# Weight blocks of a two-layer decoder trunk: a rounding load and an accumulating load in place of one plain load and two splits

## Chip, cores and metric

The kernel runs on one core of a Trainium2 chip. The metric is the device time of one execution in microseconds. Before the change it is 2004.49 us, the median of 2 runs (2004.17 and 2004.82).

## What is computed

The reference runs two layers (DEPTH = 2) on x of 512 tokens by 1024 features, all in float32. Per layer, cut to what matters:

```
h    = rms_norm(x, pre_norm[l])
proj = h @ w_in[l]            # one projection, its columns cut into ten parts
y_a  = ssd_branch(z_a, xbc, dt_raw, ...)   @ w_a[l]   # Mamba-2 SSD
y_b  = s5_branch(u_b, z_b, ..., w_glu[l])  @ w_b[l]   # S5, with a 1024x1024 GLU
y_c  = mla_branch(c_q, c_kv, k_rope, z_c, ...) @ w_c[l]  # latent attention, w_uq, w_ukv
out  = (sum of sigmoid(gate_i) * y_i) @ w_o[l]
x    = x + rms_norm(out, post_norm[l])
```

Every `@` with a weight is a dense product whose weight is read from DRAM once.

## The kernel before

TensorE multiplies in a rounded 32-bit type (`F32R`). To keep float32 accuracy every operand is held as two parts: hi, the value rounded to F32R, and lo, the value minus hi, rounded in turn. A product is then three matmuls: hi times hi, hi times lo, lo times hi.

Weights come in blocks of 128 partitions by 1024 columns (512 KB; blocks of `w_uq` and `w_ukv` have 512 columns, `w_tail` 384). `weight` (L83 to L99) prepares one block: SP issues the load of the float32 block into `wf` (L95), ScalarE writes hi into `wh` (line 59, called from L96), and VectorE, or every second or third time GpSimd (`lo_pool`, set in the attention and SSD parts), writes `wl` = `wf` - `wh` (lines 71 and 74). `wf`, `wh` and `wl` have two buffers each. `dense` (L101 to L113) then runs 16 matmuls of 128x128 by 128x512 on `wh` (L109, L110) and 8 on `wl` (L112), into one PSUM bank. `w_out` in `mix` does the same for the eight blocks of `w_o`, into tiles of their own (`woh`, `wol`) that stay for the whole of `wout`; two of these eight lie in memory that the merged sums `mg` occupy until then.

In the S5 blocks `weight` is called with a pool of its own (`sp`), once with a list of eight strided pieces of `kpad` (L93) and once with a contiguous block `odr` that the kernel itself wrote to DRAM earlier.

One layer passes through these stages; the times are those of the first layer: norm, attention with the S5 preparation as a filler (0 to 400 us), the product with `w_c` beside the S5 scan on VectorE (400 to 490), the SSD part (490 to 690), the S5 blocks with `w_a` (690 to 820), the GLU and the product with `w_b` (820 to 925), and on to `w_o` (925 to 1005).

The order of the instructions on each engine is made at build time by a scheduler that places the program's instructions one after the other as their operands and buffers come free. At run time each engine keeps that order: an instruction that waits holds up everything behind it on its own engine. DMA issues are instructions of the engine that issues them, and wait there in the same way.

Of the kernel before, what the change touches and what calls it, by code (L numbers as in the profile page):

```python
# [17 lines left out]
L = 2  # L18
T = 512
# [4 lines left out]
# first tile of each part of the input projection, in the host's order  # L24
# [10 lines left out]
class Trunk:  # L35
# [49 lines left out]
    def weight(self, src, n, pool=None):  # L85
        """hi and lo parts of a block of n columns per partition, streamed from DRAM"""
        pool = pool or self.wp
        wf = pool.tile([P, 1024], F32, name="wf", tag="wf", bufs=2)
        wh = pool.tile([P, 1024], F32R, name="wh", tag="wh", bufs=2)
        wl = pool.tile([P, 1024], F32R, name="wl", tag="wl", bufs=2)  # L90
        if isinstance(src, list):
            for rows, x in src:
                self.nc.sync.dma_start(wf[rows, :n].rearrange("p (g k) -> p g k", k=x.shape[-1]), x)  # L93
        else:
            self.nc.sync.dma_start(wf[:, :n], src)  # L95
        self.act_(wh[:, :n], wf[:, :n])  # L96
        self.nw += 1
        (self.gt if self.lo_pool and self.nw % self.lo_pool == 0 else self.tt)(wl[:, :n], wf[:, :n], wh[:, :n].bitcast(F32), ALU.subtract)
        return wh, wl  # L99

    def dense(self, src, rhs, m=P, n=None, main=True):  # L101
        """[m, T] bank of src^T rhs; rhs: (hi, lo) per 128 rows"""
        k = len(rhs)
        wh, wl = self.weight(src, k * m)
        ps = self.bank(main)
        mm = self.nc.tensor.matmul
        o = lambda i: slice(i * m, i * m + m)
        for i, (bh, bl) in enumerate(rhs):
            mm(ps[:m], wh[:, o(i)], bh, start=i == 0, stop=False)  # L109
            mm(ps[:m], wh[:, o(i)], bl, start=False, stop=False)  # L110
        for i, (bh, bl) in enumerate(rhs):
            mm(ps[:m], wl[:, o(i)], bh, start=False, stop=i == k - 1)  # L112
        return ps  # L113

    def proj2(self, l, tiles):
        """two tiles of the projection, first for the first half of the tokens"""
        w = [self.weight(self.a["w_in"][l, t], 1024) for t in tiles]
        ps = [self.bank(True) for _ in tiles]
        for half in range(2):
            tk = slice(256 * half, 256 * half + 256)  # L120
            for (wh, wl), p in zip(w, ps):
                for i, (bh, bl) in enumerate(self.h):
                    o = slice(i * P, i * P + P)
                    self.mm3(p[:, tk], wh[:, o], wl[:, o], bh[:, tk], bl[:, tk], i == 0, i == 7)
        return ps
# [48 lines left out]
    def sincos_small(self, ang, n):  # L174
# [21 lines left out]
        # sin = 2 s c, cos = 1 - 2 s^2  # L196
# [8 lines left out]
    def rsqrt_mean(self, ss, n, scale, eps=EPS):  # L205
        """(scale * ss + eps) ** -0.5 on n columns"""
        v = self.sm.tile([P, n], F32, name="rs_v", tag=f"rsv{n}")
        r = self.sm.tile([P, n], F32, name="rs_r", tag=f"rsr{n}")
        self.ts(v, ss, scale, eps, ALU.mult, ALU.add)
        self.gt(r, v, self.mhalf[:, :n], ALU.pow)  # L210
        return r

    def rsqrt_rows(self, sq, scale):
        """sq [128, T]: sums over partitions -> (scale * sum + eps) ** -0.5 along T, on every partition"""
        nc = self.nc
        ps = self.bank()
        for t in range(4):
            nc.tensor.matmul(ps[:, t:t + 1], sq[:, t * P:(t + 1) * P], self.ones[:, 0:1], start=True, stop=True)
        r = self.rsqrt_mean(ps[:, 0:4], 4, scale)
        dg = self.tmp()  # L220
        for t in range(4):
            self.ts(dg[:, t * P:(t + 1) * P], self.ident, r[:, t:t + 1], None, ALU.mult)
        pr = self.bank()
        nc.tensor.matmul(pr, self.ones, dg, start=True, stop=True)
        return pr

# [1 line left out]
    def s5_prep(self, l, pp):  # L228
# [27 lines left out]
        # f = (abar - 1) / lambda  # L256
# [18 lines left out]
        # coefficients of the scan over blocks: groups 0..31 on the lower half, 32..63 on the upper  # L275
# [25 lines left out]
        def block(b):  # L301
            """inputs in blocks of 8 steps: (step, channel of the group) on partitions; what depends on B and C alone"""
# [49 lines left out]
        def back(b, s, uf, bb, v1, w1):  # L352
# [19 lines left out]
            if s % 2:  # L372
# [3 lines left out]
                # kernel of the steps within a block  # L376
# [32 lines left out]
    def norm_in(self, tt, xt, G):  # L409
        """RMS norm of a tile of tokens (two halves of its features), transposed and split into self.hh, self.hl"""  # L410
# [15 lines left out]
    def silu2(self, l, tile_, keep=True):  # L426
        """2 silu of a tile of the projection"""
# [24 lines left out]
    def merge(self, l, i, w, acts, m, rrow=None):  # L452
        """merged += 2 sigmoid(gate_i) * (w^T acts) (* rrow along T), a tile of it; its gates run ahead"""
# [137 lines left out]
    def attend_qk(self, mp, q, k, h):  # L591
        """rows of exp(q k^T * SCALE - max), causal; their sums in self.rs"""
# [19 lines left out]
    def attend_v(self, mp, scs, v):  # L612
        """probabilities times v, transposed, as the sum of two parts of [64, T]"""
        nc = self.nc
        # key block kb holds queries kb * 128 ...
# [25 lines left out]
    def ssd_dt(self, l, sp):  # L641
        """dt, its cumulative decays and what depends on tokens and heads alone"""
# [55 lines left out]
    def ssd(self, l):  # L698
        nc, tc, a = self.nc, self.tc, self.a
        with tc.tile_pool(name=f"ssd{l}", bufs=1, reuse_waits="tile") as sp:  # L700
# [12 lines left out]
            def conv(t):  # L713
                """silu of the causal convolution of a tile of channels"""
# [16 lines left out]
            def core(g, xs, zs, bt, ct):  # L731
# [4 lines left out]
                # C B^T per chunk, keys on partitions, masked  # L736
# [7 lines left out]
                # token-major x dt, its decayed form, and B  # L744
# [26 lines left out]
                # states at the chunks' starts  # L771
# [50 lines left out]
            def head(g, hh, cbm):  # L822
                """decayed C B^T of a head, keys on partitions, and its decays along T"""
# [46 lines left out]
    def s5_scan(self, l, sp):  # L870
        """states at the starts of the blocks"""
# [14 lines left out]
    def s5_block(self, l, sp, b):  # L886
        """outputs of 8 groups, and their gelu"""
# [66 lines left out]
    def layer_in(self, l, xs):  # L954
        """xs(t): the two halves of x of a tile of 128 tokens, in SBUF"""
# [7 lines left out]
    def layer(self, l):  # L963
        nc, tc, a = self.nc, self.tc, self.a
        self.first2 = self.proj2(l, (CQ, CQ + 1))
        # rope key and dt
# [17 lines left out]
    def mix(self, l):  # L984
        nc, tc, a = self.nc, self.tc, self.a
        with ExitStack() as st:
# [6 lines left out]
            # the softmax's sums, along T  # L993
# [48 lines left out]
            def w_out(pool, k):  # L1042
                wf = self.wp.tile([P, 1024], F32, name="wf", tag="wf")
                nc.sync.dma_start(wf, a["w_o"][l, k])
                wh, wl = pool.tile([P, D], F32R, name=f"woh{k}"), pool.tile([P, D], F32R, name=f"wol{k}")
                self.split(wf, wh, wl)
                wo.append((wh, wl))
# [19 lines left out]
    def wout(self, l, mg, wo, G):  # L1067
        nc = self.nc

        def out_tile(t):  # L1070
# [18 lines left out]
            # the rows are twice the reference's: 0.5 (s / 4 + eps) ** -0.5 = (s + 4 eps) ** -0.5  # L1089
# [52 lines left out]
def _tiles(w):  # L1142
    """[L, K, M] -> [L, M / 128, 128 (row), K / 128, 128 (column)]"""
# [5 lines left out]
def layouts(i):  # L1149
# [31 lines left out]
    # constants  # L1181
# [32 lines left out]
```

## Time and profile before

| | before |
|---|---|
| median of 2 runs | 2004.49 us |
| span of the profiled execution (first to last instruction) | 2005.7 us |
| PE busy | 1890.3 us (94%) |
| DVE busy | 1451.9 us (72%) |
| ACT busy | 942.0 us (47%) |
| POOL busy | 649.9 us (32%) |
| 16 DMA engines, share | 35.4% |

The profile gives no time of the profiled execution other than its span, 1.2 us above the median of the runs. PE is TensorE, DVE VectorE, ACT ScalarE, POOL GpSimd, SP SyncE, which here only issues DMAs. Busy times of the stages are read from the view by windows, the load of the DMA engines from the DMA view, single durations from the groups by line and from the timeline.

### The profile page before, as it was taken

How to read it: one execution, taken by the hardware profiler on the slowest of the kernel's cores; microseconds unless marked ns; L12 is line 12 of the kernel's file. 1: busy time of each engine (PE TensorE's matmuls, PEld its weight loads, DVE VectorE, ACT ScalarE, POOL GpSimd, SP SyncE). 2: the span in 40 equal slices, each digit the busy share in tenths (PEclk: the TensorE clock that was granted, in tenths of full speed). 3: DMA queues.
4: the chain of work that ended last, by engine and by line, in shares of the span. 5: the costliest groups of instructions: out<-in, count | busy, mean ns of one | idle time of the engine just before them, and what ended most of it. 6: DMA issues, size and time to landing. Idle time of an engine off the chain costs nothing.

```text
span 2005.7 us, 27806 instructions
## 1 busy us (share of the span) xinstructions
PE 1890.3 (94%) x9688; PEld 1524.2 (76%) x9688; DVE 1451.9 (72%) x2845; ACT 942.0 (47%) x1743; POOL 649.9 (32%) x743
## 2 busy tenths in 40 slices
PE   7897999899999989999997999998999999999998
PEld 6685777687877868887875777776878887788786
DVE  7866667699999857744478666677999996776433
ACT  4364566522555445533333655564235563554331
POOL 1855466301333201201118556662013331012010
PEclk9898999899999999999998999998999999999999
DMA  5232234232321266344232333342332224662531
GB/s 166 88 115 83 91 118 128 83 108 74 127 74 64 75 184 181 93 152 157 88 91 83 108 104 111 91 139 82 96 123 77 74 74 111 181 171 84 168 126 42
DMA packets 132605, 219.96 MB, mean 110 GB/s; under 512 B 36208, under 2 KB 75760, under 8 KB 131952
## 3 DMA queue, kind: packets, MB, share of 16 engines
q1 hardware_dynamic: 132464, 218.19, 35.4%
q8 instruction: 76, 1.25, 0.3%
q14 instruction: 65, 0.53, 0.1%
HBM read 182.08 MB, written 31.33 MB: 106 GB/s over the span
## 4 chain that ended last, share of the span: by engine, by line
PE 59%; DVE 25%; DMA 7%; POOL 3%; ACT 3%; issue 2%; SPq 1%; DVEq 0%; POOLq 0%; ACTq 0%
PE mm L109 14%; PE mm L110 13%; PE mm L112 13%; DVE wl L71 4%; DVE keep L62 3%; PE mm L54 2%; PE mm L55 2%; PE mm L56 2%; DMA wf<-in_w_in 2%; DVE ms L882 2%; DVE sc_t L879 2%; PE pk L378 2%; DVE ms L881 1%; PE aux L55 1%; PE aux L54 1%
## 5 line engine op out<-in xcount | busy, mean ns | idle before, releaser
L109 PE MATMUL mm<-hh,wh 128*128 128x512 f32 (+1 forms) x1232 | 501.2, 407 | 16.4 <-DVE ql L71 8.8
L110 PE MATMUL mm<-hl,wh 128*128 128x512 f32 (+1 forms) x1232 | 493.6, 401 | 0.0
L59 ACT ACTIVATE wh<-wf 128x1024 fp32r<-128x1024 f32 (+1 forms) x294 | 291.2, 994 | 423.7 <-PE mm L110 240.8
L71 DVE TENSOR_TENSOR wl<-wf,wh 128x1024 fp32r<-128x1024 f32 (+1 forms) x243 | 297.5, 1229 | 183.8 <-ACT wh L59 149.6
L112 PE MATMUL mm<-hh,wl 128*128 128x512 f32 (+1 forms) x1232 | 315.1, 393 | 2.4 <-DVE wl L71 2.4
L109 PEld LDWEIGHTS mm<-hh,wh 128*128 128x128 f32 (+1 forms) x1232 | 237.2, 193 | 78.6 <-ACT wh L59 10.0
L110 PEld LDWEIGHTS mm<-hl,wh 128*128 128x128 f32 (+1 forms) x1232 | 236.8, 192 | 50.2 <-issue 1.9
L112 PEld LDWEIGHTS mm<-hh,wl 128*128 128x128 f32 (+1 forms) x1232 | 227.5, 187 | 52.0 <-DVE wl L71 3.2
L74 POOL TENSOR_TENSOR mg<-mg,tmp 128x512 f32<-128x512 f32 x32 | 77.7, 2429 | 464.4 <-DVE tmp L71 242.7
L74 POOL TENSOR_TENSOR wl<-wf,wh 128x1024 fp32r<-128x1024 f32 (+1 forms) x51 | 109.5, 2147 | 292.2 <-PE mm L112 186.7
L109 PE MATMUL mm<-ah,wh 128*128 128x512 f32 x512 | 204.1, 401 | 0.1
L110 PE MATMUL mm<-al,wh 128*128 128x512 f32 x512 | 201.2, 394 | 0.0
L112 PE MATMUL mm<-ah,wl 128*128 128x512 f32 x512 | 130.8, 396 | 0.0
L109 PEld LDWEIGHTS mm<-ah,wh 128*128 128x128 f32 x512 | 96.2, 188 | 25.5 <-issue 1.8
L110 PEld LDWEIGHTS mm<-al,wh 128*128 128x128 f32 x512 | 96.2, 188 | 22.1 <-issue 0.5
L112 PEld LDWEIGHTS mm<-ah,wl 128*128 128x128 f32 x512 | 95.7, 188 | 22.6
L602 DVE CUSTOM_DVE_ANT_0 sc<-aux,cmask 128x128 f32<-128x128 f32 (+3 forms) x128 | 60.3, 486 | 50.8 <-PE aux L56 49.1
L59 ACT ACTIVATE sc<-sc,nm 128x128 f32<-128x128 f32 (+3 forms) x128 | 70.3, 553 | 30.3 <-DVE nm L66 30.2
L74 POOL TENSOR_TENSOR pv<-pq,ar 128x288 f32<-128x288 f32 x64 | 56.4, 903 | 85.3 <-PE pk L378 68.3
L71 DVE TENSOR_TENSOR pl<-aux,ph 128x512 fp32r<-128x512 f32 (+1 forms) x96 | 54.8, 594 | 26.2 <-ACT ph L59 25.7
L59 ACT ACTIVATE tmp<-mm 128x512 f32<-128x512 f32 x76 | 44.9, 594 | 60.6 <-PE mm L56 34.1
L62 DVE SCALAR_TENSOR_TENSOR keep<-mm,cw,keep 128x511 f32<-128x511 f32 (+2 forms) x96 | 71.1, 741 | 2.1 <-ACT keep L59 1.5
(344 smaller groups left out, 4079.9 us busy)
## 6 DMA issues: line engine op xcount, KB each, us to landing
wf<-in_w_in SPq DMA_DIRECT2D x156, 512.0 KB
odr<-pv SPq DMA_DIRECT2D x64, 128.0 KB
wf<-in_w_c SPq DMA_DIRECT2D x16, 512.0 KB
wf<-in_w_a SPq DMA_DIRECT2D x16, 512.0 KB
wf<-kpad SPq DMA_DIRECT2D x128, 64.0 KB
wf<-odr SPq DMA_DIRECT2D x16, 512.0 KB
wf<-in_w_glu SPq DMA_DIRECT2D x16, 512.0 KB
wf<-in_w_b SPq DMA_DIRECT2D x16, 512.0 KB
```

What stands on the lines that cost most here:

```text
L54: mm(out, ah, bh, start=start, stop=False)
L55: mm(out, ah, bl, start=False, stop=False)
L56: mm(out, al, bh, start=False, stop=stop)
L59: self.nc.scalar.activation(out, in_, func, **kw)
L62: self.nc.vector.scalar_tensor_tensor(out, in0, s, in1, op0, op1)
L71: self.nc.vector.tensor_tensor(out, a, b, op)
L74: self.nc.gpsimd.tensor_tensor(out, a, b, op)
L109: mm(ps[:m], wh[:, o(i)], bh, start=i == 0, stop=False)
L110: mm(ps[:m], wh[:, o(i)], bl, start=False, stop=False)
L112: mm(ps[:m], wl[:, o(i)], bh, start=False, stop=i == k - 1)
L378: nc.tensor.matmul(pk.rearrange("p g k -> p (g k)"), bbp[b % 2][:, q:q + 4].rearrange("p g h -> p (g h)"), v1[:, :, 0:8].rearrange("p g k ...
L602: nc.vector.tensor_tensor_reduce(out=sc, in0=ps[:, :n], in1=self.cmask[:, 512 - n:512], op0=ALU.add, op1=ALU.max, scale=1.0, scalar=-3.0e3 ...
```

## The change

For a block that is not given as a list, `wf` disappears. GpSimd issues a DMA from DRAM into `wh`, whose type differs from the source's, so that the DMA itself rounds. ScalarE writes `wl` = -1 times `wh`. GpSimd issues a second DMA of the same block from DRAM into `wl` that adds to what is there. VectorE and GpSimd no longer subtract for such blocks. `wh` and `wl` have three buffers in the common pool, two in the pool of the S5 blocks. The list of `kpad` pieces is prepared as before, always by VectorE. `w_out` is changed in the same way.

```
     def weight(self, src, n, pool=None):
+        nc, bufs = self.nc, 2 if pool else 3
         pool = pool or self.wp
-        wf = pool.tile([P, 1024], F32, name="wf", tag="wf", bufs=2)
-        wh = pool.tile([P, 1024], F32R, name="wh", tag="wh", bufs=2)
-        wl = pool.tile([P, 1024], F32R, name="wl", tag="wl", bufs=2)
+        wh = pool.tile([P, 1024], F32R, name="wh", tag="wh", bufs=bufs)
+        wl = pool.tile([P, 1024], F32R, name="wl", tag="wl", bufs=bufs)
         if isinstance(src, list):
+            wf = pool.tile([P, 1024], F32, name="wf", tag="wf", bufs=2)
             for rows, x in src:
-                self.nc.sync.dma_start(wf[rows, :n].rearrange("p (g k) -> p g k", k=x.shape[-1]), x)
-        else:
-            self.nc.sync.dma_start(wf[:, :n], src)
-        self.act_(wh[:, :n], wf[:, :n])
-        self.nw += 1
-        (self.gt if self.lo_pool and self.nw % self.lo_pool == 0 else self.tt)(wl[:, :n], wf[:, :n], wh[:, :n].bitcast(F32), ALU.subtract)
+                nc.sync.dma_start(wf[rows, :n].rearrange("p (g k) -> p g k", k=x.shape[-1]), x)
+            self.act_(wh[:, :n], wf[:, :n])
+            self.tt(wl[:, :n], wf[:, :n], wh[:, :n].bitcast(F32), ALU.subtract)
+            return wh, wl
+        nc.gpsimd.dma_start(wh[:, :n], src)
+        self.act_(wl[:, :n], wh[:, :n].bitcast(F32), scale=-1.0)
+        nc.gpsimd.dma_start(wl[:, :n], src, accum_op=ALU.add)
         return wh, wl
...
             def w_out(pool, k):
-                wf = self.wp.tile([P, 1024], F32, name="wf", tag="wf")
-                nc.sync.dma_start(wf, a["w_o"][l, k])
                 wh, wl = pool.tile([P, D], F32R, name=f"woh{k}"), pool.tile([P, D], F32R, name=f"wol{k}")
-                self.split(wf, wh, wl)
+                nc.gpsimd.dma_start(wh, a["w_o"][l, k])
+                self.act_(wl, wh.bitcast(F32), scale=-1.0)
+                nc.gpsimd.dma_start(wl, a["w_o"][l, k], accum_op=ALU.add)
                 wo.append((wh, wl))
```

In all 294 blocks go this way (278 through `weight`, 16 through `w_out`; 40 of them are of 512 columns and 2 of 384), so 588 DMA issues now stand on GpSimd, where none stood.

What stands on POOL before, in the SSD part of the second layer, names with their numbers: subtractions of weight blocks between the small additions and products of the SSD core (`stf` is the running state, `er` and `ssq` belong to the output, `xef` is the decayed input).

```order
L74 TENSOR_TENSOR wl_15484<-wf_15482,wh_15483 128x1024 [waits DMAHW0_49,PE_49,Activation_49]
L74 TENSOR_TENSOR stf_15354<-stf_15354,dec_14939 128x256 [waits DMAHW5_49,DVE_49]
L74 TENSOR_TENSOR stf_15354<-stf_15354,dec_14939 128x256 [waits DVE_49]
L74 TENSOR_TENSOR wl_15657<-wf_15655,wh_15656 128x1024 [waits DMAHW2_49,PE_49,Activation_49]
L74 TENSOR_TENSOR tmp_15412<-tmp_15412,er_15413 128x384 [waits DVE_49]
L74 TENSOR_TENSOR tmp_15528<-tmp_15528,er_15529 128x384 [waits DVE_49]
L74 TENSOR_TENSOR ssq_14957<-ssq_14957,tmp_15573 128x512 [waits Activation_49]
L74 TENSOR_TENSOR wl_15782<-wf_15780,wh_15781 128x1024 [waits DMAHW4_49,PE_49,Pool_49]
```

And now, at the same place: line 98 is the rounding load of a block, line 100 the adding load of the same block.

```order
L100 DMA wl_15268<-in_w_in 128x1024 [waits DMASW1_49,PE_49,Activation_49]
L98 DMA wh_15388<-in_w_in 128x1024 [waits DMASW2_49,PE_49]
L100 DMA wl_15389<-in_w_in 128x1024 [waits DMASW3_49,PE_49,Activation_49]
L98 DMA wh_15438<-in_w_in 128x1024 [waits DMASW4_49,PE_49]
L74 TENSOR_TENSOR stf_15140<-stf_15140,dec_14733 128x256 [waits DMAHW7_49,DMAHW0_49,DVE_49]
L74 TENSOR_TENSOR stf_15140<-stf_15140,dec_14733 128x256 [waits DVE_49]
L100 DMA wl_15439<-in_w_in 128x1024 [waits DMASW5_49,PE_49,Activation_49]
```

Each block now takes two places on POOL, and the second follows the first directly: of the 294 blocks 175 have no other rounding load between their two DMAs, 94 have one, 25 more than one. The small products stand behind them.

What stands on SP before, among the S5 blocks of the first layer: line 95 are the weight loads, line 93 the strided pieces of `kpad`.

```order
L95 DMA wf_7418<-odr0_568 128x1024 [waits DMAHW3_49,DVE_49]
L95 DMA wf_7711<-in_w_a 128x1024 [waits DMAHW4_49,DVE_49]
L894 DMA uf_7594<-u20_570 128x512 [waits DMAHW5_49,DVE_49]
L95 DMA wf_7761<-in_w_in 128x1024 [waits DMAHW6_49,DVE_49]
L93 DMA wf_7606<-kpad0_567 16x8x128 [waits DMAHW2_49,DMAHW1_49,DMAHW7_49,DMAHW0_49,DVE_49]
L93 DMA wf_7606<-kpad0_567 16x8x128
L894 DMA sf_7600<-sdr0_4583 128x1x512 [waits DVE_49]
L93 DMA wf_7606<-kpad0_567 16x8x128
```

And on POOL now, among the same S5 blocks, with the additions into the merged sums `mg` between:

```order
L98 DMA wh_7663<-in_w_in 128x1024 [waits DMASW7_49,PE_49]
L100 DMA wl_7615<-in_w_a 128x1024 [waits DMASW0_49,Activation_49]
L100 DMA wl_7664<-in_w_in 128x1024 [waits DMASW1_49,PE_49,Activation_49]
L98 DMA wh_7779<-in_w_in 128x1024 [waits DMASW2_49,PE_49]
L98 DMA wh_7327<-odr0_565 128x1024 [waits DMASW3_49,PE_49]
L100 DMA wl_7780<-in_w_in 128x1024 [waits DMASW4_49,DMASW5_49,PE_49,Activation_49]
L98 DMA wh_7811<-in_w_a 128x1024 [waits PE_49]
L100 DMA wl_7328<-odr0_565 128x1024 [waits DMASW6_49,Activation_49]
L74 TENSOR_TENSOR mg2_4137<-mg2_4137,tmp_7415 128x512 [waits DVE_49]
```

The loads of `in_w_in`, `in_w_a` and `odr` have left SP, where the `kpad`, `uf` and `sf` transfers remain, and each stands on POOL twice.

## Rows read from the trace of the kernel before

**Rows 1.** The page: spans, busy time, chain by engine.

```profile
span 2005.7 us, 27806 instructions
...
PE 1890.3 (94%) x9688; PEld 1524.2 (76%) x9688; DVE 1451.9 (72%) x2845; ACT 942.0 (47%) x1743; POOL 649.9 (32%) x743
...
PE 59%; DVE 25%; DMA 7%; POOL 3%; ACT 3%; issue 2%; SPq 1%; DVEq 0%; POOLq 0%; ACTq 0%
```

**Rows 2.** Windows, first layer: us, busy PE PEld DVE ACT POOL, PEclk, DMA share, GB/s.

```profile
0.00:400.00 400.00, 349.66 (x1730) 280.69 (x1730) 276.94 (x606) 208.56 (x484) 214.58 (x308) 0.93 0.37 108
400.00:490.00 90.00, 90.00 (x396) 72.18 (x396) 86.05 (x305) 22.84 (x28) 4.83 (x2) 1.00 0.28 101
490.00:690.00 200.00, 192.89 (x1048) 154.73 (x1048) 187.19 (x308) 108.05 (x176) 62.57 (x42) 1.00 0.24 82
690.00:820.00 130.00, 123.86 (x803) 101.86 (x802) 88.23 (x103) 63.79 (x90) 15.56 (x9) 0.99 0.61 166
820.00:925.00 105.00, 104.91 (x495) 84.29 (x494) 54.77 (x59) 45.37 (x55) 17.33 (x5) 1.00 0.38 131
```

**Rows 3.** PE's waits: line, releaser, total us, times, longest us.

```profile
PE mm L109 <- DVE ql L71: 8.8, 6, 4.2
...
PE mm L109 <- ACT wh L59: 6.6, 2, 3.6
PE mm L55 <- POOL wl L74: 5.8, 1, 5.8
...
PE mm L112 <- DVE wl L71: 2.4, 2, 1.3
```

**Rows 4.** Groups by line, shapes apart: xcount | busy us, mean ns | idle before.

```profile
L71 DVE TENSOR_TENSOR wl<-wf,wh 128x1024 fp32r<-128x1024 f32 x217 | 276.6, 1280 | 165.9 <-ACT wh L59 141.6 <-PE mm L112 9.6 <-ACT tmp L59 5.8
L59 ACT ACTIVATE wh<-wf 128x1024 fp32r<-128x1024 f32 x252 | 265.0, 1056 | 358.3 <-PE mm L110 197.6 <-DMA wf<-in_w_in 44.0 <-DMA wf<-kpad 27.0
...
L74 POOL TENSOR_TENSOR wl<-wf,wh 128x1024 fp32r<-128x1024 f32 x35 | 88.1, 2516 | 272.3 <-PE mm L112 175.2 <-ACT wh L59 64.7 <-PE aux L750 16.7
...
L74 POOL TENSOR_TENSOR pv<-pq,ar 128x288 f32<-128x288 f32 x64 | 56.4, 903 | 85.3 <-PE pk L378 68.3 <-PE aux L55 9.5 <-DVE ar L71 5.9
```

**Rows 5.** The same windows, instructions that read wf alone: DVE, ACT, POOL.

```profile
0.00:400.00 400.00, 40.24 (x35) 41.65 (x48) 20.24 (x12) 0.93 0.37 108
490.00:690.00 200.00, 21.68 (x16) 28.28 (x27) 31.93 (x12) 1.00 0.24 82
```

**Rows 6.** DMA from 400 to 490 us: packets, MB, share of 16 engines.

```profile
q1 hardware_dynamic: 2245, 9.00, 27.7%
```

**Rows 7.** DMA from 690 to 820 us, and issues by line.

```profile
q1 hardware_dynamic: 15152, 21.51, 60.9%
...
wf<-in_w_in SPq DMA_DIRECT2D x11, 512.0 KB
...
wf<-odr SPq DMA_DIRECT2D x8, 512.0 KB
wf<-in_w_a SPq DMA_DIRECT2D x7, 512.0 KB
```

**Rows 8.** Issues by line from 820 to 925 us.

```profile
wf<-in_w_glu SPq DMA_DIRECT2D x8, 512.0 KB
wf<-in_w_in SPq DMA_DIRECT2D x5, 512.0 KB
wf<-in_w_b SPq DMA_DIRECT2D x5, 512.0 KB
wf<-in_w_o SPq DMA_DIRECT2D x4, 512.0 KB
```

**Rows 9.** One load on an idle DMA: its issue on SP, its reader on ACT.

```profile
936.98 0.33 SPq L1044 DMA_DIRECT2D wf<-in_w_o  x1
...
940.34 1.06 ACT L59 ACTIVATE woh<-wf 128x1024 fp32r<-128x1024 f32 x1 [0.93 <-DMA wf<-in_w_o]
```

**Rows 10.** Timeline: a small POOL instruction.

```profile
1970.54 0.56 POOL L74 TENSOR_TENSOR rs_r<-rs_v,mhalf 128x1 f32<-128x1 f32 x1 [13.57 <-DVE rs_v L68]
```

## What the change will do to the time

> **What bounds the kernel now.** I read the page first, then busy time by stage, then PE's waits, then the cost of the weight preparation, and last the DMA engines, which the change loads most.
>
> The page shows PE busy 94% of the span and 59% of the chain of waits on it, with VectorE 25% [rows 1]. So 2005.7 - 1890.3 = 115.4 us of PE idle is all that any relief can win. By stage this idle time is uneven: 50 us lie in the attention stage (0 to 400), 7 in the SSD stage, 6 in the S5 blocks and next to none in the product with `w_c` and in the GLU stage [rows 2]. PE waited for the weight preparation itself hardly at all: 6.6 us for a hi part, 5.8 and 2.4 us for lo parts in the three largest such groups, against 8.8 us for one split of the attention's queries [rows 3]. The preparation is large on the engines, small on the path: 276.6 us of VectorE, 265.0 of ScalarE and 88.1 of GpSimd for full blocks [rows 4]. VectorE is at 187 of 200 us in the SSD stage [rows 2], but PE is at 193 there, so VectorE's relief can return no more than PE's 7 us per layer.
>
> What is new must be carried by the DMA engines and by GpSimd's queue. The DMA engines are at 0.24 to 0.38 in most stages, but at 0.61 in the S5 blocks [rows 2, 7]. GpSimd is at 215 of 400 us in the attention stage and at 63 of 200 in the SSD stage [rows 2].
>
> **The change part by part.**
>
> *Removed work.* ScalarE stays level: its hi copy of 1056 ns [rows 4] becomes a negation of the same size, in the same memory and types of 32 bits. VectorE loses its 1280 ns per block, GpSimd its 2516 ns where it had the block [rows 4]. In the attention stage that is at most 40 us of VectorE and 20 of GpSimd, in the SSD stage 22 and 32 [rows 5]; PE's own waits for them are the few us above. I credit 4 us per layer in the attention stage and, since PE is nearly full there, nothing in the SSD stage.
>
> *DMA time of a block.* From 400 to 490 us 9.00 MB took 27.7% of 90 us [rows 6], that is 24.9 us, or 2.77 us per MB. A block of 0.524 MB so takes 1.45 us of the 16 engines. The rounding load moves the same bytes; I take 1.45 us again, with 2.9 as the upper bound if the conversion halves the rate. The adding load is in no row. Its lower bound is one load, 1.45 us. It fetches the block from DRAM and the negative from SBUF and writes one result, so two fetches stand for one: 2.9 us, which I take, because the fetch of the negative is as many bytes as the other and no row shows a transfer whose bytes come free. The Trainium skill (Collectives: The Full Stack, "The bandwidth ceiling: the fold count and why AG ≠ RS ≠ AR") says the same of an add inside the DMA engines: the addition is free, but two source reads share one read ring and so halve the rate. By that rule the adding load costs 2.9 us, by the row of a plain load 1.45; no run here shows it yet.
>
> *S5 blocks, 690 to 820 us.* The queue was busy 60.9% of 130 us, 79.2 us, with 11 + 8 + 7 = 26 loads that now become two [rows 7]; the strided `kpad` blocks stay as they are. 26 x 2.9 = 75.4, in all 154.6 us of DMA work in a stage of 130. With three buffers (two in the S5 pool) little of it can be fetched ahead, so the stage takes 24.6 us longer. At 1.45 us the sum is 116.9, 90% of the stage, and PE waits only now and then: 3 us.
>
> *GLU and `w_b`, 820 to 925 us.* 0.38 x 105 = 40 us of DMA [rows 2] and 8 + 5 + 5 + 4 = 22 loads [rows 8] give 40 + 63.8 = 104 of 105 us. It just fits; for a queue that full I charge two loads of delay, 3 us. In the stage of `w_c` 16 blocks give 25 + 46 = 71 of 90 us, which is hidden.
>
> *GpSimd's queue in the SSD stage.* Here the order puts the adding load right behind the rounding load of the same block, almost throughout, with the small SSD products behind both. One pass of GpSimd through a block is then: issue c, landing, negation, issue c. From the issue of a load on an idle DMA to its reader's start were 940.34 - 936.98 = 3.36 us, of which 0.33 the issue [rows 9]: 3.03. With 1.06 for the negation a pass is 4.09 + 2c. The other GpSimd work of the stage is 62.6 - 31.9 = 30.7 us [rows 2, 5] over 16 + 12 = 28 blocks [rows 5], 1.1 us each. A block has 200 / 28 = 7.14 us. So the queue holds as long as 5.19 + 2c stays under 7.14, that is c under 0.98 us. No row shows a DMA issued by GpSimd. Its smallest instruction takes 0.56 us [rows 10], its subtraction of a block 2.5 [rows 4]; SP's issue of 0.33 [rows 9] is the lowest bound. I take 0.9 us, the product over 288 elements [rows 4], as the nearest to writing some 256 descriptors. Then a pass is 6.99 of 7.14 us: at its edge, and the waits of those small products for VectorE now stand in one line with it. I charge 0.3 us per block, 8 us per layer. The additions that wait behind the pass feed the SSD matmuls, so this delay is PE's.
>
> *GpSimd's queue in attention.* By the code this stage has 4 + 1 + 2 + 8 + 8 + 12 + 8 = 43 blocks. GpSimd keeps 214.6 - 20.2 = 194 us [rows 2, 5], and gets 86 issues of 0.9, 77 us. In about half of the blocks nothing stands between the two DMAs, and the queue is blocked for 3.03 + 1.06 us: 22 x 4.09 = 90. Together 361 of 400 us. The S5 preparation that PE transposes hangs on this queue and loses its slack. I charge 12 us per layer, a quarter of the idle time that PE already has there, less the 4 of relief: 8 net.
>
> *The buffers.* The third buffer replaces the depth that `wf` gave. A rounding load waits until PE has left the hi part three blocks earlier. The 16 blocks of the `w_c` stage in 90 us [rows 2] are 5.6 us each, so it has over two blocks, some 13 us, to land, and the lo part three, 16.8 us. The chain to the lo part is 3.03 + 1.06 + 2c, and 3.03 + 1.45 for the slower adding load, about 10.4 us: hidden, as long as no neighbour blocks the queue. The last two `w_o` blocks can no longer be loaded into `wf` ahead of time and wait for the memory of `mg`; the matmuls on the first six cover most of that, and I charge 1 us per layer.
>
> *Sum.* Per layer 24.6 + 3 + 8 + 8 + 1 = 44.6; two layers 89 us. 2005.7 + 89 = 2095 in the span. The span of the profiled execution lies 1.2 us above the median, so I forecast **2094 us**.
>
> **The rivals.**
>
> *Hidden (no change).* The adding load costs 1.45 us and GpSimd's issue 0.56. Then the S5 blocks are 90% full (+3), the GLU stage is at 72 of 105, an SSD pass is 6.3 of 7.14 us, and the relief of VectorE stands: -4 in attention, -3 in SSD. 2 x (3 - 4 - 3 + 1) = -6: about 2000 us. For it speaks the low DMA share in most stages, against it the 0.61 in the S5 blocks.
>
> *Faster.* VectorE's relief shortens the chain of attention, and PE's idle time shrinks. It decides from 41 us on, over a third of the 115.4 us of idle. All of PE's waits in the three weight groups make 14.8 us [rows 3]; the other 26 would have to come from VectorE waits such as that for `ql`, whose engine would go from 277 to 237 of 400 us. And neither queue may cost anything. That gives about 1962 us.
>
> *Every converted byte at half rate.* The rounding load too costs 2.9 us. Then a block costs 5.8 where it cost 1.45. S5 blocks: 79.2 + 26 x 4.35 = 192, +62; GLU: 40 + 22 x 4.35 = 136, +31; with the other terms, 17, 110 per layer: 2005.7 + 220, about 2225 us. A GpSimd issue of 2.4 us would do as much by another way, with an SSD pass of 10.0 us where 7.14 are free: 28 x 2.8 = 80 us per layer in that stage alone.
>
> **How the numbers follow.** Forecast 0.46 (2045 to 2150), hidden 0.27 (1985 to 2045), faster 0.07, half rate or dear issue 0.20. About 2% is what a measurement of this kernel can tell from no change, 1964 to 2045 us. That makes 0.07 faster, 0.27 same and 0.66 slower. The likeliest case is the forecast, so the predicted time is its sum. The range leaves out the faster case and the upper half of the dear one: 1985 to 2230 us. The forecast's own range is 2045 to 2150.
>
> **What would show it.** In the profile after: the DMA share of the S5 blocks near 0.95 or above and that stage near 155 us; packets of the adding load that take about twice those of a load; GpSimd's issues near 0.9 us each; PE's waits in the S5 blocks for DMA of `wh` or `wl`, which are not there now; in the SSD stage PE waiting for SSD products that wait for GpSimd. The forecast is wrong if the adding load is as cheap as a plain one (then the S5 blocks stay at 130 us), if GpSimd's issue is below 0.6 us (then the SSD stage stays at 200), or if stages that I hold hidden, `w_c` and `w_o`, grow.

## The result, and the profile after

The changed kernel takes 2334.65 us, the median of two runs (2332.89 and 2336.41), against 2004.49: a ratio of 1.164, 95% interval 1.160 to 1.168. The prediction was 2094 us, slower by 89; it is slower by 330, above the range of 1985 to 2230.

The page of the changed kernel: the span, the busy time of each engine, the DMA queues (q0 is the one of GpSimd's issues, new here; q1 that of SP's) and the shares of the chain of waits by engine, to be read against [rows 1].

```profile
span 2330.8 us, 28075 instructions
PE 1999.6 (86%) x9688; PEld 1595.8 (68%) x9688; DVE 1143.4 (49%) x2602; ACT 933.1 (40%) x1743; POOL 893.1 (38%) x1280
...
q0 software_dynamic: 84672, 286.04, 55.3%
q1 hardware_dynamic: 90128, 75.17, 11.6%
...
PE 28%; DMA 26%; issue 25%; POOL 11%; DVE 5%; ACT 3%; SPq 1%; POOLq 0%; DVEq 0%; ACTq 0%
```

PE holds 28% of the chain where it held 59%; DMA, issue and GpSimd together hold 62%. The 9688 matmuls are the same, but PE is busy 109 us longer and idle 2330.8 - 1999.6 = 331 us instead of 115. So 216 of the 325 us in the span are new idle time, and 109 are matmuls that ran slower: the mean granted clock is 0.92, where it was 0.97.

For the comparison by stage the kernels are cut at the same instructions, not at the round times of [rows 2]: attention (with the norm, in the second layer also `w_o` of the first) ends at the first matmul of `w_c`; `w_c` where its last matmul of hi by hi starts; the SSD stage at the first matmul of `w_a`; the S5 blocks at the last S5 product; the GLU and `w_b` where the last matmul of hi by hi of `w_b` starts; the tail is the rest. The view by windows for three stages of the first layer, before and after (busy us and number of instructions of PE, weight load, DVE, ACT, POOL; granted clock; DMA share; GB/s). Before:

```profile
470.50:687.70 217.20, 210.09 (x1130) 168.38 (x1129) 203.63 (x364) 112.75 (x183) 63.54 (x42) 1.00 0.24 83
687.70:826.80 139.10, 132.96 (x878) 109.50 (x876) 93.99 (x108) 66.68 (x94) 19.23 (x11) 0.99 0.59 160
826.80:965.40 138.60, 138.51 (x608) 111.40 (x607) 65.84 (x69) 54.72 (x65) 22.92 (x8) 1.00 0.40 137
```

After, the same three, and below them 50 us of the second layer's GLU and `w_b` stage:

```profile
509.40:755.40 246.00, 221.80 (x1133) 179.45 (x1132) 166.00 (x311) 111.99 (x184) 70.80 (x89) 0.94 0.60 136
755.40:973.20 217.80, 176.54 (x985) 142.48 (x984) 67.20 (x91) 77.90 (x107) 62.25 (x71) 0.88 0.81 185
973.20:1118.00 144.80, 121.81 (x501) 96.59 (x499) 20.46 (x29) 43.41 (x53) 44.70 (x59) 0.91 0.83 204
2200.00:2250.00 50.00, 43.48 (x171) 34.82 (x170) 2.75 (x4) 8.99 (x10) 16.56 (x20) 0.88 1.02 231
```

SSD: 29 us longer with the DMA engines busy 60%. S5 blocks: 79 us longer at a share of 0.81. About 107 matmuls of the S5 window stood in the GLU window before, so those two stages are best taken together: 277.7 us before, 362.6 after.

The two largest groups of PE's waits in that SSD window, after (line, what it waited for: us in total, times, longest):

```profile
PE aux L54 <- DVE stf L71: 6.0, 4, 2.2
PE mm L114 <- DMA wl<-in_w_c: 6.0, 1, 6.0
```

The second is the last lo part of `w_c`, whose eight matmuls lie behind the cut. They end 2.5 us behind it before and 10.4 us after. Counted to their end, `w_c` is 15 us longer than before in the first layer and 16 in the second, and the SSD stage 21 and 28.

All kernels of this study by these cuts, from the traces, in us, first layer / second layer:

| kernel | attention | w_c | SSD | S5 blocks | GLU, w_b | tail | span |
|---|---|---|---|---|---|---|---|
| before | 390/418 | 80/80 | 217/210 | 139/140 | 139/138 | 54 | 2005.7 |
| after | 422/458 | 87/87 | 246/246 | 218/218 | 145/143 | 60 | 2330.8 |
| e1 second DMA overwrites | 388/431 | 84/80 | 205/209 | 181/188 | 126/128 | 56 | 2077.8 |
| e2 link cut | 401/437 | 81/82 | 212/212 | 194/194 | 150/151 | 55 | 2167.7 |
| e3 both | 378/412 | 82/82 | 212/212 | 166/165 | 138/139 | 56 | 2041.5 |
| e4 second DMA one block later | 399/442 | 88/87 | 205/206 | 205/195 | 145/146 | 56 | 2174.1 |
| e5 two ScalarE steps | 417/460 | 84/89 | 225/223 | 218/223 | 146/145 | 57 | 2285.6 |
| e6 first load by SP | 432/466 | 84/83 | 206/207 | 207/206 | 148/150 | 60 | 2248.6 |
| e7 before, issued by GpSimd | 396/431 | 80/81 | 213/213 | 152/147 | 145/143 | 57 | 2056.3 |
| e8 before, six slots | 405/428 | 79/80 | 224/214 | 164/164 | 149/149 | 54 | 2109.4 |
| e9 six slots, SSD changed | 402/428 | 83/80 | 202/202 | 163/163 | 149/150 | 56 | 2079.8 |
| e10 SSD changed, one later | 389/419 | 80/80 | 205/205 | 141/139 | 139/138 | 56 | 1991.2 |
| e11 SSD changed, in order | 390/423 | 80/79 | 233/235 | 141/143 | 138/138 | 56 | 2056.6 |
| e12 S5 and GLU changed, in order | 393/419 | 80/80 | 220/221 | 207/218 | 128/119 | 55 | 2137.7 |
| e13 S5 and GLU changed, one later | 391/417 | 80/80 | 213/215 | 198/204 | 135/127 | 55 | 2113.7 |

How a pass of GpSimd runs in the SSD stage shows in its timeline (start, duration, instruction, in brackets the idle time before it and what ended it):

```profile
602.85 0.85 POOL L100 DMA_DIRECT2D wl<-in_w_in  x1 [6.97 <-ACT wl L59]
603.41 0.85 POOL L98 DMA_DIRECT2D wh<-in_w_in  x1
603.97 1.32 POOL L74 TENSOR_TENSOR tmp<-tmp,er 128x384 f32<-128x384 f32 x1
608.58 1.32 POOL L74 TENSOR_TENSOR tmp<-tmp,er 128x384 f32<-128x384 f32 x1 [3.28 <-DVE er L71]
611.49 0.87 POOL L100 DMA_DIRECT2D wl<-in_w_in  x1 [1.59 <-ACT wl L59]
...
627.64 0.88 POOL L100 DMA_DIRECT2D wl<-in_w_in  x1 [5.62 <-ACT wl L59]
628.23 0.86 POOL L98 DMA_DIRECT2D wh<-in_w_in  x1
```

and in the chain of waits of the same stretch (start, us, what):

```profile
602.85 0.55 POOL wl L100
603.41 6.70 DMA wh<-in_w_in
610.11 0.02 issue
610.13 1.07 ACT wl L59
611.20 0.29 issue
611.49 0.80 POOL wl L100
```

The adding load of one block and the rounding load of the next are issued 0.56 us apart. In the trace's packets the adding load then runs first, from 604.1 to about 607.6 us, and the bulk of the rounding load only behind it, to 609.3. Its landing, 6.7 us after its issue, starts the negation (1.07), and that the next adding load at 611.49: 8.64 us from one to the next.

### The profile page after: what moved, and what is told of

Read it like the earlier page. It is cut to its first block, busy times and chain, and to the rows that moved or that the text cites. A ratio compares the mean times of both kernels' runs of the same rounds, so it can differ in the third digit from the quotient of the medians.

```text
span 2330.8 us, 28075 instructions
## 1 busy us (share of the span) xinstructions
PE 1999.6 (86%) x9688; PEld 1595.8 (68%) x9688; DVE 1143.4 (49%) x2602; ACT 933.1 (40%) x1743; POOL 893.1 (38%) x1280
## 3 DMA queue, kind: packets, MB, share of 16 engines
q0 software_dynamic: 84672, 286.04, 55.3%
## 4 chain that ended last, share of the span: by engine, by line
PE 28%; DMA 26%; issue 25%; POOL 11%; DVE 5%; ACT 3%; SPq 1%; POOLq 0%; DVEq 0%; ACTq 0%
DMA wh<-in_w_in 9%; PE mm L114 6%; PE mm L111 6%; PE mm L112 5%; POOL wl L100 3%; DMA wf<-kpad 3%; POOL wh L98 2%; DMA bc<-in_s_bc 2%; DMA wl<-in_w_in 2%; POOL pv L74 2%; PE mm L55 2%; DMA wl<-in_w_b 2%; PE mm L54 2%; PE mm L56 1%; ACT wl L59 1%
## 5 line engine op out<-in xcount | busy, mean ns | idle before, releaser
L59 ACT ACTIVATE wl<-wh 128x1024 fp32r<-128x1024 f32 (+1 forms) x278 | 275.7, 993 | 811.7 <-DMA wh<-in_w_in 376.4
L112 PE MATMUL mm<-hl,wh 128*128 128x512 f32 (+1 forms) x1232 | 502.6, 408 | 0.0
L114 PE MATMUL mm<-hh,wl 128*128 128x512 f32 (+1 forms) x1232 | 337.4, 408 | 26.9 <-DMA wl<-in_w_in 26.8
L100 POOL DMA_DIRECT2D wl<-in_w_in x156 | 137.3, 882 | 520.8 <-ACT wl L59 459.6
L112 PE MATMUL mm<-al,wh 128*128 128x512 f32 x512 | 209.6, 412 | 0.0
L114 PE MATMUL mm<-ah,wl 128*128 128x512 f32 x512 | 143.9, 424 | 24.8 <-DMA wl<-in_w_c 17.5
L98 POOL DMA_DIRECT2D wh<-in_w_in x156 | 116.7, 748 | 106.2 <-PE mm L112 71.6
L62 DVE SCALAR_TENSOR_TENSOR tmp<-tmp,mm 128x512 f32<-128x512 f32 x16 | 11.0, 687 | 158.2 <-PE mm L114 158.2
L62 DVE SCALAR_TENSOR_TENSOR keep<-tmp,keep 128x512 f32<-128x512 f32 x48 | 38.0, 792 | 92.3 <-ACT tmp L59 92.3
L74 POOL TENSOR_TENSOR mg<-mg,tmp 128x512 f32<-128x512 f32 x32 | 57.0, 1782 | 38.7 <-DVE tmp L71 23.1
```

What stands on the lines that cost most here:

```text
L59: self.nc.scalar.activation(out, in_, func, **kw)
L62: self.nc.vector.scalar_tensor_tensor(out, in0, s, in1, op0, op1)
L74: self.nc.gpsimd.tensor_tensor(out, a, b, op)
L98: nc.gpsimd.dma_start(wh[:, :n], src)
L100: nc.gpsimd.dma_start(wl[:, :n], src, accum_op=ALU.add)
```

## The theories, and the experiments

In the sessions of the experiments the kernel before took 2006.6 to 2008.2 us; ratios are to the runs of the same session.

**Theory A.** The loss is a chain on GpSimd's queue: the adding load waits for the negation, the negation for the rounding load, and the rounding load stands behind the adding load of the block before, on GpSimd and in the DMA queue. **Theory B.** The bytes: the DMA engines are full. **Theory C.** The 588 issues cost GpSimd too much. A packet of 4096 bytes takes 174 ns (median) in a rounding load and 328 in an adding load, where a plain load before had 159.

One caution holds for all that follows. An edit changes what the build-time scheduler sees, and so the order on all engines. e1 has row for row the order of the changed kernel, on every engine; in e10 to e13 the stages that are not edited stay within 5 us of before, but for the second SSD stage of e12 (11 us longer). In e2 to e9 the order differs more, and a part of their difference is that.

**e1, the second DMA overwrites.**

```
-        nc.gpsimd.dma_start(wl[:, :n], src, accum_op=ALU.add)
+        nc.gpsimd.dma_start(wl[:, :n], src)
```

> The second DMA of a block overwrites wl instead of adding to it (so the lo part is the rounded block, and the subtraction is left out). Order on every engine is that of the changed kernel, and the second DMA still waits for ScalarE's negation. In the changed kernel a packet of the first DMA takes 174 ns and one of the second 328 ns, so this takes 8 x 154 ns = 1.23 us of the DMA engines from each block. Theory A (the chain on GpSimd's queue: the second DMA waits for the negation, the negation for the first DMA's landing, and the first DMA stands behind the second DMA of the block before, on GpSimd and in the DMA queue): the 1.23 us are in the chain, so the SSD stage goes from 246 to about 212 us (28 blocks), the S5 blocks from 218 to about 186 (26 blocks), in all about 2180 us. Theory B (the DMA engines are full): only the S5 blocks and the GLU stage, with a DMA share of 0.8, gain; the SSD stage with a share of 0.60 stays at 246; S5 about 160; in all about 2200 us. Theory C (the issues themselves cost GpSimd too much): no change, about 2330 us.

Measured: 2079.6 us, ratio to before 1.035 [1.033, 1.037], 255 us under the changed kernel, more than either theory said. GpSimd's queue (q0) falls in the page from 55.3% of 2330.8 us to this share:

```profile
span 2077.8 us, 28075 instructions
...
q0 software_dynamic: 84672, 286.04, 46.0%
```

That is 1289 - 956 = 333 us of DMA time less, and 255 of them are won. In the SSD stage the engines were busy 60%, so bytes alone could not bind there, and yet it falls from 246 to 205 and 209 us, 41 and 37 us for 30 blocks (7808 packets of 4096 bytes, 256 to a block): all of each block's 1.23 us are in the chain. In the S5 blocks 37 us are won in the first layer and 30 in the second, again about 1.2 and 1.0 us for each of 30 blocks. Theory C falls as the main cause: the issues are all still there.

**e2, the link cut; e3, both edits.** ScalarE writes zeros from a constant of one column (`mhalf`) instead of -`wh`:

```
-        self.act_(wl[:, :n], wh[:, :n].bitcast(F32), scale=-1.0)
+        self.act_(wl[:, :n], self.mhalf[:, 0:1].broadcast_to([P, n]), scale=0.0)
```

> ScalarE writes zeros into wl from a constant, with as much work, instead of the negative of wh; the second DMA still adds the block to it (the lo part is the rounded block, the subtraction is left out). All DMA packets and all issues stay; only the link from the first DMA's landing to the second DMA's issue is gone. Theory A: GpSimd no longer waits 6 to 7 us per block; the SSD stage returns to about 215 us, attention to about 400, the S5 blocks to about 160, which the DMA engines need; in all about 2080 us. Theory B: the bytes are the same, so the S5 blocks stay near 218 and the total near 2330, at best 2280. Theory C: about 2330 us.

> Both of the two edits before: zeros from a constant, and a second DMA that overwrites (the lo part is the rounded block, the subtraction is left out). Two loads of 1.4 us per block remain, both issued by GpSimd, with no wait between them. Theory A: within 2% of the time before, about 2020 us. Theory B: the same as with the overwriting second DMA alone, about 2200 us. Theory C: about 2330 us, since the 588 issues remain.

Measured: e2 2167.6 us (1.079 [1.077, 1.081]), e3 2043.5 us (1.019 [1.016, 1.022]). With e1 and the changed kernel that makes a square:

| | second DMA adds | second DMA overwrites | difference |
|---|---|---|---|
| waits for the negation | 2334.65 | 2079.6 | 255 |
| does not wait | 2167.6 | 2043.5 | 124 |
| difference | 167 | 36 | |

Of the 330 us, 39 are left when neither is there (two loads without an add per block, both issued by GpSimd), 36 come with the wait alone, 124 with the adding alone, and 131 only with the two together: a slow transfer inside a chain. In the SSD stage, where the engines have room, cutting the wait is enough (212 us with either load). In the S5 and GLU stages it is not: 344 us in e2, 304 in e3, for 278 before. There B is right in good part, and A's sum for e2, 2080 us, was 88 too low.

**e4, one later.** An edge at build time, which orders without a semaphore, puts the adding load behind the next block's rounding load:

```
+        if self.lastl is not None:
+            self.tc.add_manual_dep(self.lastl.ins, h.ins.name, NoSync)
         self.act_(wl[:, :n], wh[:, :n].bitcast(F32), scale=-1.0)
-        nc.gpsimd.dma_start(wl[:, :n], src, accum_op=ALU.add)
+        self.lastl = nc.gpsimd.dma_start(wl[:, :n], src, accum_op=ALU.add)
```

> The changed kernel with an edge at build time that puts the second DMA of each block behind the first DMA of the next block on GpSimd; nothing else changes. Theory A: the wait for landing and negation is covered by a whole pass, and the first DMA no longer stands behind the second in the DMA queue; the SSD stage falls from 246 to about 215 us, the S5 blocks from 218 to about 175, in all about 2130 us. Theory B and C: about 2330 us, since bytes and issues are the same.

Measured: 2181.4 us, 1.086 [1.084, 1.089]; same bytes, same computation, 153 us faster than the changed kernel. A's SSD stage came out, and a little more (205 us for 215); its S5 blocks did not (205 and 195 for 175), and its sum was 51 us too low. The largest group of GpSimd's waits in the SSD stage (line, what it waited for: us in total, times, longest), in the changed kernel and then in e4, there with the group that was the largest:

```profile
POOL wl L100 <- ACT wl L59: 101.8, 23, 7.0
```

```profile
POOL wh L98 <- PE mm L114: 70.3, 19, 5.6
...
POOL wl L102 <- ACT wl L59: 14.5, 4, 5.4
```

Now GpSimd waits mostly for PE to give a buffer back, and little for the block's own preparation. The median time to landing of the rounding load falls with it (KB each, us), in the changed kernel and in e4:

```profile
wh<-in_w_in POOLq DMA_DIRECT2D x29, 512.0 KB, 6.2
```

```profile
wh<-in_w_in POOLq DMA_DIRECT2D x29, 512.0 KB, 4.3
```

**e5, two ScalarE steps.** A copy of `wh` into `wl` ahead of the negation.

> The changed kernel with ScalarE's step made twice as long: a copy of wh into wl and then the negation of wl in place, about 1.06 us more per block, before the second DMA. ScalarE is busy 40% of the span of the changed kernel, so as work this is hidden. Theory A (the chain of landing, negation and second DMA sets the pass of GpSimd's queue, 8.1 us per block in the SSD stage): every pass that binds grows by 1.06 us: the SSD stage from 246 to about 277 (30 blocks), the S5 blocks by about 25, attention by some 15, in all about 2480 us. Theory B (the DMA engines are full): 2335 to 2350 us.

Measured: 2283.0 us, 1.137 [1.135, 1.139]: faster than the changed kernel, against both theories' numbers. The edit did not only make the chain longer. To the scheduler the adding load now came later, and it placed other rounding loads ahead of it: of the 278 blocks of `weight` those with no other rounding load between their two DMAs are 93, where they were 173. The test is spoilt as a price of 1.06 us; order and length moved together, against each other. It fits A that the gain lies in the SSD stage (225 us for 246), but it doesn't show it.

**e6, first load by SP.** `wf` by SP and `wh` by ScalarE as before, `wl` by negation and adding load; two buffers.

> The hi part made as before the change (SP loads wf, ScalarE rounds it into wh); ScalarE writes wl = -wh and GpSimd issues the adding DMA; two buffers each. Bytes and adding DMAs are those of the changed kernel; the first load leaves GpSimd's queue and the DMA queue in which the adding transfers stand. Theory A: a block's first load no longer waits for the block before; the SSD stage falls to 210 to 220 us, the S5 blocks to about 180, in all about 2130 us. Theory B: near 2330, with the S5 blocks unchanged at about 218 us.

Measured: 2248.5 us, 1.119 [1.117, 1.122]. The SSD stage falls as A said (206), the S5 blocks only to 207, and attention is longer still than in the changed kernel (432/466). The sum of A was 120 us too low; with two buffers and one more copy of ScalarE per block this kernel has limits of its own, which were not taken apart.

**e7, issues alone.** The kernel before, `nc.sync.dma_start` to `nc.gpsimd.dma_start` in its plain weight loads.

> The kernel before with one edit: its plain weight loads into wf are issued by GpSimd and not by SP; ScalarE and VectorE split as before (GpSimd still has its share of the subtractions). It prices the 294 issues of about 0.86 us on GpSimd and its in-order queue without a second transfer. Theory A: within 2.5% of the time before, 2010 to 2050 us. Theory C (GpSimd's issues are what costs): 5% or more over the time before, above 2100 us.

Measured: 2060.6 us, 1.027 [1.025, 1.029], 10 us over the upper end of A and far under C. GpSimd as the issuer costs this kernel some 52 us with one plain load per block, in attention, S5 and GLU.

**e8, six slots; e9, SSD alone on them.** `wf`, `wh` and `wl` share six slots (one tag for the three); e9 adds the two DMAs, one block later, in the SSD stage.

> The kernel before with one edit: wf, wh and wl share six slots of one size in place of two each, so that a slot that wf gives back early can hold a later block. No DMA is added. Theory A: PE waited only some 15 us for the weight preparation, so 1985 to 2010 us, 0 to 1% faster. A rival (more depth alone would have paid): under 1970 us.

> The six shared slots of the run beside it, and in the SSD stage alone the two DMAs of the change, with the second DMA of a block put behind the first of the next one; everywhere else the kernel before. Theory A: the SSD stage goes as in the run with that order, about 205 us where the kernel before has 217 and 210, because VectorE and GpSimd lose the subtractions there and the DMA engines have room; in all 8 to 16 us below the run with six slots alone, about 1985 to 1995 us. Theory B (any adding DMA costs): slower than six slots alone by 10 us or more.

Measured: e8 2117.5 us, 1.055 [1.053, 1.057]; e9 2082.3 us, 1.037 [1.035, 1.039]. e8 missed: shared slots make no DMA and no arithmetic, and cost 5%, about half of it in the S5 blocks (164). Why was not followed; it shows how much the order alone is worth here. Beside it e9 wins 35 us, where A said 8 to 16; 22 and 11 of them lie in the two SSD stages.

**e10, SSD alone, one later; e11, SSD alone, in order.** The slots of before; in the SSD stage the pairs rotate through those of `wh` and `wl` and, every third block, the two of `wf`; the last two lines shown are not in e11:

```
+        if self.dmap and pool is self.wp:
+            t = ("wh", "wl") if self.nd % 3 < 2 else ("wf", "wf")
...
+            h = nc.gpsimd.dma_start(wh[:, :n], src)
+            if self.lastl is not None:
+                self.tc.add_manual_dep(self.lastl.ins, h.ins.name, NoSync)
```

> The kernel before, with the two DMAs of the change in the SSD stage alone; its pairs of tiles there rotate through the slots of wh and wl and, every third block, through the two slots of wf. The second DMA of a block stands behind the first of the next block. Theory A: DMA engines have room there (0.24 before) and the waits are covered, so the SSD stage takes 202 to 206 us where it had 217 and 210; in all 1985 to 1998 us. Theory B: slower than before by 10 us or more. A rival (what the order of the other stages does outweighs it): outside 1985 to 2010 us with the SSD stage at 202 to 206 all the same.

> The run beside it without the edge: in the SSD stage the second DMA of a block mostly follows its own first one, as in the changed kernel. Theory A: one pass of GpSimd is again some 8 us per block, so the SSD stage takes about 240 us and the whole 2050 to 2075 us. Theory B (bytes): the same time as the run beside it.

Measured: e10 1993.7 us, ratio 0.9928 [0.9914, 0.9941], 0.7% under the kernel before: clear of the interval, but less than the 2% from which the forecast counted a change; e11 2061.2 us, 1.027 [1.025, 1.028]. The edits differ in the order of two DMAs per block in one stage; with it the scheduler has put other instructions in 1442 of PE's 9688 places and 486 of VectorE's 2818. That stage by windows, in e10 and then in e11:

```profile
469.60:674.30 204.70, 204.70 (x1130) 168.92 (x1128) 173.37 (x344) 113.14 (x183) 66.03 (x81) 1.00 0.69 157
```

```profile
469.90:702.50 232.60, 215.25 (x1097) 174.10 (x1096) 173.42 (x341) 110.19 (x181) 66.10 (x80) 0.96 0.57 136
```

and the largest group of GpSimd's waits there, in e10 and in e11 (in these files the two loads stand in lines 94 and 98):

```profile
POOL wh L94 <- PE mm L122: 71.9, 19, 5.9
```

```profile
POOL wl L98 <- ACT wl L59: 116.6, 24, 8.5
```

In e10 PE is busy for the whole stage, at full clock, with the DMA engines at 0.69. For the SSD stage this pair, with e1, whose order is that of the changed kernel, shows A: same bytes, same issues, same buffers; 205 us with the wait covered, 233 without. Against the kernel before, e10 also has a third pair of tiles in that stage. No run has that pair alone, so how much of the 14 us is due to it stays open.

**e12, S5 and GLU alone, in order; e13, one later.** The same construction for the S5 blocks and the GLU product.

> The kernel before, with the two DMAs of the change in the S5 blocks and the GLU product alone (pairs rotating through the slots of wh and wl and, every third block, of wf; two pairs for the S5 pool). Theory A: the S5 blocks grow by themselves as in the changed kernel, from 139 to 205 to 220 us, and the other stages stay within 3 us; in all 2140 to 2170 us. A rival (the growth there was brought in by the late state in which the SSD stage leaves the queues): under 190 us for the S5 blocks, under 2110 in all.

> The run beside it with the second DMA of a block put behind the first of the next one. If the DMA engines alone set these stages (some 297 us of transfers in the S5 and GLU stages of a layer, DMA share 0.95 or more), this and the run beside it give the same time. If it is the queue, which leaves the engines idle (share 0.8), the share rises and the S5 blocks fall by 10 to 25 us per layer: 2100 to 2130 us in all.

Measured: e12 2139.5 us, 1.066 [1.064, 1.068]; e13 2116.6 us, 1.055 [1.054, 1.057]. Most of the growth arises in these stages themselves: S5 blocks, GLU and `w_b` together take 334.7 and 336.6 us in the two layers of e12, for 277.7 and 277.8 before and 362.6 and 361.2 in the changed kernel, whose `w_b` and `w_o` loads are changed too. The other stages did not all stay within 3 us (the second SSD stage is 11 longer). The total of e13 and its S5 blocks lie where the queue was to put them, but the order is worth little there: the stages together take 332.7 and 331.1 us, 2 and 6 less than in e12, and of the 23 us between the two kernels 13 lie in the SSD stages, which were not edited. The S5 blocks by windows, e12 and then e13:

```profile
692.60:899.50 206.90, 168.77 (x973) 135.99 (x972) 69.60 (x93) 79.15 (x108) 59.96 (x71) 0.91 0.83 192
```

```profile
683.90:882.10 198.20, 165.39 (x973) 133.17 (x972) 70.61 (x92) 77.46 (x106) 59.21 (x70) 0.90 0.85 195
```

Neither reaches 0.95, so it is not engines that are simply full, and neither gains much by the order. The S5 blocks go more with the transfer time, at a share of 0.77 to 0.85 in the first layer of all of e1 to e4, e12, e13 and the changed kernel.

## Why the prediction was wrong

**Right:** the direction, the DMA time of a block, GpSimd's issue, and the places. The adding load's packets take 2.06 times those of a plain load (328 to 159 ns), the rounding load's 1.09 times: 2.62 and 1.39 us by medians, where 2.9 and 1.45 were taken. By the rule of the Trainium skill that was weighed there (Collectives: The Full Stack, "The bandwidth ceiling: the fold count and why AG ≠ RS ≠ AR") the add needs two source reads and so has half the rate. The factor 2.06 agrees; that a second read is the reason no run here shows. The issue, taken as 0.9 us, is 0.81 (477.5 us for 588), and the next one starts 0.55 to 0.6 us after it:

```profile
L100 POOL DMA_DIRECT2D wl<-in_w_in x156 | 137.3, 882 | 520.8 <-ACT wl L59 459.6 <-ACT sth L59 19.3 <-ACT stf L59 13.6
L98 POOL DMA_DIRECT2D wh<-in_w_in x156 | 116.7, 748 | 106.2 <-PE mm L112 71.6 <-PE mm L56 18.9 <-PE pm L363 4.7
```

The rivals fall with this: the rounding load is not at half rate and the issue is not 2.4 us, so the 2225 of that rival is nearer for a wrong reason; hidden and faster are refuted by the time, though e10 shows that both are there in one stage.

**GpSimd's queue in the SSD stage: forecast +8 per layer, measured +29 and +36** (21 and 28 without the last lo part of `w_c`). The step that failed is the landing of 3.03 us, read from a load on an idle queue [rows 9]. It is 6.2 us after the issue, since the adding load of the block before, 2.6 us, is on the way in the same queue; without the add it lands after 4.5 us (e1), with the adding load behind it after 4.3 (e4). That transfer was priced, and left out of the pass. With it the pass is 0.55 (issue) + 6.2 + 1.06 + 0.3 = 8.1 us, above the 7.14 us that a block had, and 30 blocks make 243 us of the 246. The small products, added as 1.1 us per block, lie inside the wait and cost nothing. The Trainium skill (DMA: Bandwidth & Descriptors, "SWDGE vs HWDGE vs iDMA") says that DMAs issued by GpSimd have only one queue between them, which an engine drains packet by packet; the order of the packets above agrees. Read with the order on GpSimd, it puts the adding load of one block ahead of the rounding load of the next.

**S5 blocks, GLU and `w_b`: forecast +24.6 and +3, measured +85 and +83.** The work was right. By the forecast's own prices the new cuts hold 139 us (0.50 of 277.7) and 57 loads (7296 packets of 4096 bytes) at 2.9, 304 us; measured are 0.82 x 362.6 = 297. What failed is that this work would run at a share of 1 ("It just fits"). The engines can run fuller: in the 50 us at 2200 above, just after the loads for six pairs of `w_o` tiles were issued, with eight of GpSimd's DMAs on the way at their start, they are at 1.02 (the share adds up packet times, and these can overlap on an engine). In these stages they stay at 0.82, with 0.87 in e2 and e4 and 0.83 to 0.85 in the S5 blocks of e12 and e13. In the S5 blocks of the changed kernel these are GpSimd's largest wait and then PE's two largest:

```profile
POOL wl L100 <- ACT wl L59: 123.8, 26, 8.7
```

```profile
PE pM L54 <- DMA wh<-odr: 16.0, 6, 4.5
PE pM L55 <- DMA wl<-odr: 15.6, 6, 5.6
```

For 124 of 218 us GpSimd issues nothing more, and 32 of PE's 41 us of idle there are waits for the two loads of `odr`, whose pool has two pairs of buffers. The forecast had named such waits as its sign. That few blocks are in flight, two or three pairs, is the nearest reason for the share. Counted in the trace from issue to landing, GpSimd has at most one DMA on the way for 25% of the stage, at a share of 0.51, two for 36% at 0.88, and three or four for 39% at 0.94. But no run had room for more blocks, so it is argued and not shown, and the cause of the 0.82 stays open.

**Attention: forecast +8 net, measured +32, and +40 in the second layer with `w_o` and the norm.** The first layer's stage issues 48 blocks, where the forecast counted 43. The relief was undersized and so was the load: in e3 the stage falls to 378 and 412, 12 and 6 us under before, while the adding (e2) takes back 22 and 25 and the wait another 21 and 22. The sizes carry the caution on the order.

**`w_c` and `w_o`: forecast hidden and +1, measured +7 and +6** (`w_c` +15 with its last lo part). The text named them as what would prove it wrong if they grew. `w_c` is back at 81 and 82 us without the wait (e2): its condition "as long as no neighbour blocks the queue" did not hold.

**The clock was not in the sum.** The forecast counted only waits. Here 216 us of new waits came with 109 us of slower matmuls: in the S5 blocks, the GLU and `w_b` of the first layer PE was busy 271 of 278 us at granted clocks of 0.99 and 1.00, and is now busy 298 of 363 at 0.88 and 0.91, a mix of its levels of 2.4 and 1.2 GHz. So a microsecond of new idle time cost half a microsecond more, on the average of this kernel.

## What to carry to other kernels

When a transfer is to wait for another one's result, write out the pass of the queue that issues both, with every transfer that stands ahead of it in that queue and not the landing on an idle one; then ask for the order that covers the wait with the next block. A conversion or an addition that the DMA does paid here only where the engines had room (0.24 in the SSD stage) and the order was right: in the better order the SSD stage was 4% shorter (e10), and the S5 blocks with the GLU and `w_b` 20% longer (e13). DMA work near 100% of a stage did not just fit; in the S5 and GLU stages here it ran at 0.82.

## What the runs showed of the hardware

The rounding of a float32 block on its way costs little: 174 ns per packet against 159, and a plain load takes 159 by GpSimd's issue too (e7). In the stretch shown, GpSimd's DMAs ran one behind the other: by medians of the SSD stage a rounding load landed after 6.2 us behind an adding load, and after 4.3 with that one behind it. Where PE's busy share fell, its granted clock fell too: in the S5 blocks from 96% busy at 0.99 to 81% at 0.88, by the windows above.
